# Low parts written over the raw weights, and rings of six raw and four high units, in a two-layer hybrid decoder

## The chip, the cores and the metric

The kernel runs on one core of one Trainium2 chip. A core has TensorE (PE in the profile; PEld is its loading of weights), VectorE (DVE), ScalarE (ACT), GpSimd (POOL), SyncE (SP, which here only starts transfers), 16 DMA engines, an on-chip memory for operands and eight banks for sums of products. The metric is the device time of one execution in microseconds (us), the median of three runs.

## The reference

Two decoder layers over 256 positions of width 2048, all float32:

```python
def reference(x, ...):
    for layer in range(2):
        xn = rms_norm(x, norm_mix[layer])
        if layer % 2 == 0:
            x = x + mixer_mlstm_ssd(xn, *mixer_params[layer])   # (xn @ w_in), mLSTM and SSD heads, then (mixed @ w_out)
        else:
            x = x + mixer_moba(xn, *mixer_params[layer])        # (xn @ w_qkv), attention, then (o @ w_o)
        x = x + swiglu(rms_norm(x, norm_ffn[layer]), *ffn_params[layer])
    return rms_norm(x, final_norm)

def swiglu(x, w_gate, w_up, w_down):
    return (jax.nn.silu(x @ w_gate) * (x @ w_up)) @ w_down
```

The weights are nearly all of the work: w_in is 2048 x 12336, w_out 4096 x 2048, w_qkv 2048 x 6144, w_o 2048 x 2048, and each layer has w_gate and w_up of 2048 x 5632 and w_down of 5632 x 2048.

## The kernel before

**Products.** TensorE multiplies in a rounded 32-bit form (fp32r). To keep float32 accuracy each operand is split into a high part (the rounded value) and a low part (the value less its high part), and a product is the sum of three: high by high, high by low, low by high (lines 479, 480 and 481 in `add`; 387 and 391 in `lin_w`; 417 to 419 in `lin_a`). One matmul is 128 x 128 by 128 x 512. Activations are split once and stay; weights are read once, in strips of 512 columns, and split as they come.

**What happens to a unit of weights.** In `block`, which does the gate z, w_out, the value columns of w_qkv, w_o and all of the two FFNs, a unit is four tiles of 128 x 512 (two row tiles of two strips, 8 KB a partition). `weights` (line 433) starts its two transfers of 512 KB on SyncE's queue into a `raw` buffer, ScalarE casts it to the high part `wh` (line 445) and VectorE subtracts that from `raw` into the low part `wl` (line 447), each in two pieces of 1024 columns. The letters of a plan say how each unit is multiplied. "P" is a plain unit: 24 matmuls. "S" is a unit of sums, seven products in place of eight: VectorE first makes four sums of the raw tiles (lines 454, 455, 457), which are a unit of their own in the raw ring; three of the raw tiles are split (one cast and one subtraction of 1536 columns), and all four sums (in two pieces of 1024 again); 21 matmuls follow. `chunks` (line 347) does the same for `lin_w` and `lin_a` in half units of 1024 columns.

**Rings.** From the stage z on the buffers are rings of three for each of `raw`, `wh` and `wl`, with one more raw buffer (`rawx`) for every fourth raw unit in the stages z, f and g (function `unit`, line 123). In the mixer the rings are four half units of raw and three each of `wh` and `wl`. A raw buffer is free for the next transfer once its cast and its subtractions are done; a `wh` or `wl` buffer once TensorE has read it.

**Order.** The kernel is written tile by tile, and the order on each engine is settled when it is built: an instruction goes where its dependencies and its priority put it (`tc.high_priority` moves casts, subtractions and evictions forward). Each engine then runs its list in order, and waits where an operand is not there.

**Stages.** m: the strips of w_in for the mLSTM and SSD heads, with the heads' own work between the strips. z: the gate columns of w_in, then w_out. f: FFN of layer 0. a: attention, w_qkv and w_o. g: FFN of layer 1. An FFN runs over its 11 strips of hidden columns in groups of 4, 4 and 3: `hidden` for each strip of the group (gate and up together), then `add_blocks` (line 918) for the group's part of w_down, twice 1024 output columns. The place where a group goes from its last hidden strip to w_down is called a seam here; there are six. At the end of a block's last unit of sums, lines 525 to 532 read the banks `acc_e` of the products into `pre`.

The lines that set the buffers before:

```python
MIXER = ({"raw": 4, "wh": 3, "wl": 3}, ...)
STAGING = tuple({tag: 1} for tag in "raw1 raw2 wh1 wh2 wl1 raw0 wh0 wl0 wl2".split())
...
    turn[kind] = turn.get(kind, -1) + 1
    return held_tile(f"{kind}{turn[kind] % 3}", shape, name, dt)
```

Of the kernel before, what the change touches and what calls it, by code (L numbers as in the profile page):

```python
# [43 lines left out]
STAGING = tuple({tag: 1} for tag in "raw1 raw2 wh1 wh2 wl1 raw0 wh0 wl0 wl2".split())  # L44
MIXER = ({"raw": 4, "wh": 3, "wl": 3}, {"cb": 1}, {"rows": 3}, {"hm": 2}, {"gap": 192}, {"ba": 4}, {"cols": 2}, {"wide": 2}, {"rb": 1})
JOIN = ({"rawx": 1}, {"gap": 256}, {"blk": 2})
FFN = ({"rawx": 1}, {"skh": 3}, {"blk": 4}, {"pre": 1})
ATTN = ({"blk": 4}, {"qk": 4}, {"v": 2}, {"rope": 1, "mask": 1}, {"rb": 1})
# [18 lines left out]
def hybrid_trunk(ctx: ExitStack, tc: tile.TileContext, a: dict, out: bass.AP):  # L67
# [8 lines left out]
    tmp = ctx.enter_context(tc.tile_pool(name="tmp", bufs=9))  # L76
    psm = ctx.enter_context(tc.tile_pool(name="psm", bufs=1, space=PSUM))
# [6 lines left out]
    staging = []  # L84

    def open_pool(name, pools):
        for i, tags in enumerate(pools):
            guard = tc.tile_pool(name=f"{name}{i}", bufs=1, reuse_waits="tile")
            pool = guard.__enter__()
            if "gap" in tags:  # L90
                pool.tile([P, tags["gap"] // 4], F32, name="gap")
            yield guard, pool, tags
# [6 lines left out]
    def open_stage(name, pools):  # L99
# [8 lines left out]
        stage["spare"] = any("rawx" in tags for tags in pools)  # L108

    def open_staging():  # L110

        close_stage()
        for guard, pool, tags in open_pool("st", STAGING):
            ctx.callback(guard.__exit__, None, None, None)
            staging.append((pool, tags))

    def held_tile(tag, shape, name, dt=F32):
        for pool, tags in stage["pools"] + staging:
# [4 lines left out]
    def unit(kind, shape, name, dt=F32):  # L123

        if not staging:
            return held_tile(kind, shape, name, dt)
        if kind == "raw" and stage["spare"]:
            turn["spare"] = turn.get("spare", -1) + 1
            if turn["spare"] % 4 == 3:
                return held_tile("rawx", shape, name, dt)  # L130
        turn[kind] = turn.get(kind, -1) + 1
        return held_tile(f"{kind}{turn[kind] % 3}", shape, name, dt)
# [214 lines left out]
    def chunks(w, col, nk, lead=None):  # L347

        n = 4 if staging else KC
        for k in range(0, nk, KC):  # L350
            if k % n == 0:
                raw = unit("raw", [P, n, STRIP], "raw")
                wh = unit("wh", [P, n, STRIP], "wh", F32R)
                wl = unit("wl", [P, n, STRIP], "wl", F32R)
# [888 lines left out]
```

## Time and profile before

| | |
|---|---|
| median of three runs | 2555.2 us (2554.48 to 2555.55) |
| span of the profiled execution | 2552.6 us |
| DMA packets | 507.49 MB, mean 199 GB/s |
| busy time of ScalarE | 1488.6 us (58%) |
| line 445, cast from raw, all shapes | 563 casts, 623.6 us |
| line 445, cast from sums | 250 casts, 256.9 us |
| line 447, low part from raw, all shapes | 563 subtractions, 740.5 us |
| line 447, low part from sums | 250 subtractions, 298.2 us |
| line 373, low part of half units | 223 subtractions, 269.6 us |
| lines 454, 455, 457, the sums of raw tiles | 125 of each; 152.1, 85.3 and 85.3 us |

The execution that was profiled has no time of its own beside its span; the 2.6 us between its span and the median of the runs are what lies around the span. A line of the profile names a group of instructions: source line, engine, operation, output and inputs, shape, count, busy time and mean duration in ns, and then the engine's idle time just before them with what ended it. Durations run from the start of an instruction to its last write, and two instructions on one engine overlap: what an instruction takes of its engine is the distance from its start to the next one's.

### The profile page before, as it was taken

How to read it: one execution, taken by the hardware profiler on the slowest of the kernel's cores; microseconds unless marked ns; L12 is line 12 of the kernel's file. 1: busy time of each engine (PE TensorE's matmuls, PEld its weight loads, DVE VectorE, ACT ScalarE, POOL GpSimd, SP SyncE). 2: the span in 40 equal slices, each digit the busy share in tenths (PEclk: the TensorE clock that was granted, in tenths of full speed). 3: DMA queues.
4: the chain of work that ended last, by engine and by line, in shares of the span. 5: the costliest groups of instructions: out<-in, count | busy, mean ns of one | idle time of the engine just before them, and what ended most of it. 6: DMA issues, size and time to landing. Idle time of an engine off the chain costs nothing.

```text
span 2552.6 us, 32527 instructions
## 1 busy us (share of the span) xinstructions
PE 2539.5 (99%) x12147; PEld 2122.4 (83%) x12147; DVE 2222.0 (87%) x2751; ACT 1488.6 (58%) x1960; POOL 55.7 (2%) x105
## 2 busy tenths in 40 slices
PE   9999999999999999999999999999999999999998
PEld 8888888888888888888888888888888888888887
DVE  5776778798989999999999987767999999999998
ACT  6455665566656655565555655666565545555555
POOL 1000010000000000000000000000000000000000
PEclk9999999999999999999999999999999999999999
DMA  8666576566565656565656557554556566665664
GB/s 291 176 208 185 164 230 185 167 205 214 181 214 177 221 188 218 203 223 174 230 191 222 195 173 231 165 165 147 195 181 219 191 213 207 211 201 198 223 205 165
DMA packets 257022, 507.49 MB, mean 199 GB/s; under 512 B 16104, under 2 KB 16256, under 8 KB 256352
## 3 DMA queue, kind: packets, MB, share of 16 engines
q1 hardware_dynamic: 249952, 483.20, 58.0%
q0 software_dynamic: 5616, 19.53, 2.2%
q10 hardware_dynamic: 1296, 2.69, 0.3%
q8 instruction: 95, 1.56, 0.2%
q14 instruction: 63, 0.52, 0.1%
HBM read 494.76 MB, written 2.14 MB: 195 GB/s over the span
## 4 chain that ended last, share of the span: by engine, by line
PE 95%; DVE 2%; issue 1%; ACT 1%; DMA 1%; SPq 0%; POOL 0%; POOLq 0%; ACTq 0%; DVEq 0%
PE acc_f L479 19%; PE acc_f L480 19%; PE acc_f L481 19%; PE acc_w L387 11%; PE acc_w L391 6%; PE acc_e L479 4%; PE acc_e L481 4%; PE acc_e L480 4%; PE acc_a L417 2%; PE acc_a L418 2%; PE acc_a L419 2%; PE p_tr L279 1%; PE p_y L891 1%; DVE wl L373 0%; PE p_num L768 0%
## 5 line engine op out<-in xcount | busy, mean ns | idle before, releaser
L445 ACT CAST wh<-raw 128x1024 fp32r<-128x1024 f32 (+1 forms) x563 | 623.6, 1147 | 384.0 <-PE acc_f L481 292.8
L447 DVE TENSOR_TENSOR wl<-raw,wh 128x1024 fp32r<-128x1024 f32 (+1 forms) x563 | 740.5, 1337 | 84.9 <-ACT wh L445 81.5
L479 PE MATMUL acc_f<-wh,x 128*128 128x512 f32 x1086 | 424.8, 391 | 0.5 <-DVE xres L928 0.5
L481 PE MATMUL acc_f<-wh,x 128*128 128x512 f32 x1086 | 422.9, 389 | 0.0
L480 PE MATMUL acc_f<-wl,x 128*128 128x512 f32 x1086 | 422.7, 389 | 0.0
L445 ACT CAST wh<-sums 128x1024 fp32r<-128x1024 f32 x250 | 256.9, 1052 | 282.5 <-PE acc_f L481 147.1
L373 DVE TENSOR_TENSOR wl<-raw,wh 128x1024 fp32r<-128x1024 f32 x223 | 269.6, 1222 | 128.9 <-ACT wh L372 125.2
L372 ACT CAST wh<-raw 128x1024 fp32r<-128x1024 f32 x223 | 230.6, 1048 | 183.7 <-PE acc_w L387 94.5
L447 DVE TENSOR_TENSOR wl<-sums,wh 128x1024 fp32r<-128x1024 f32 x250 | 298.2, 1218 | 10.6 <-ACT wh L445 9.8
L479 PEld LDWEIGHTS acc_f<-wh,x 128*128 128x128 f32 x1086 | 203.9, 188 | 43.9 <-DVE pre L1029 1.3
L481 PEld LDWEIGHTS acc_f<-wh,x 128*128 128x128 f32 x1086 | 203.9, 188 | 42.5
L480 PEld LDWEIGHTS acc_f<-wl,x 128*128 128x128 f32 x1086 | 203.9, 188 | 41.7
L387 PE MATMUL acc_w<-xa,wh 128*128 128x512 f32 x768 | 207.8, 398 | 1.2 <-DVE xa L222 1.1
L387 PEld LDWEIGHTS acc_w<-xa,wh 128*128 128x128 f32 x768 | 139.3, 189 | 27.4 <-ACT wh L365 1.4
L454 DVE TENSOR_TENSOR sums<-raw 128x1024 f32<-128x1024 f32 x125 | 152.1, 1217 | 8.4 <-DMA raw<-in_l_ffn_up 3.2
L387 PE MATMUL acc_w<-x,wh 128*128 128x512 f32 x512 | 139.2, 399 | 0.0
L391 PE MATMUL acc_w<-xa,wl 128*128 128x256 f32 x768 | 121.2, 283 | 0.0
L391 PEld LDWEIGHTS acc_w<-xa,wl 128*128 128x128 f32 x768 | 109.6, 190 | 6.5
L387 PEld LDWEIGHTS acc_w<-x,wh 128*128 128x128 f32 x512 | 92.5, 189 | 16.9
L479 PE MATMUL acc_e<-wh,skx 128*128 128x512 f32 x261 | 101.7, 391 | 0.0
L480 PE MATMUL acc_e<-wl,skx 128*128 128x512 f32 x261 | 101.6, 389 | 0.0
L481 PE MATMUL acc_e<-wh,skx 128*128 128x512 f32 x261 | 101.6, 389 | 0.0
(356 smaller groups left out, 4657.8 us busy)
## 6 DMA issues: line engine op xcount, KB each, us to landing
raw<-in_l_w_in SPq DMA_DIRECT2D x191, 512.0 KB, 3.7
raw<-in_l_ffn_gate SPq DMA_DIRECT2D x176, 512.0 KB, 4.0
raw<-in_l_ffn_up SPq DMA_DIRECT2D x176, 512.0 KB, 4.9
raw<-in_l_ffn_down SPq DMA_DIRECT2D x176, 512.0 KB, 5.0
raw<-in_l_w_qkv SPq DMA_DIRECT2D x96, 512.0 KB, 4.7
raw<-in_l_w_out SPq DMA_DIRECT2D x64, 512.0 KB, 5.0
raw<-in_l_w_o SPq DMA_DIRECT2D x32, 512.0 KB, 4.7
hr<-h POOLq DMA_DIRECT2D x32, 256.0 KB, 2.8
```

The costliest lines, as they stand in the source:

```text
L372: nc.scalar.copy(wh[:, ks, :], raw[:, ks, :])
L373: nc.vector.tensor_sub(wl[:, ks, :], raw[:, ks, :], wh[:, ks, :].bitcast(F32))
L387: return nc.tensor.matmul(banks[f], wh[:, kk, f * P:(f + 1) * P], kt.both(k0 + kk), start=k0 + kk == 0, stop=False, skip_group_check=True)
L391: nc.tensor.matmul(banks[f][:, :T], wl[:, kk, f * P:(f + 1) * P], kt.parts(k0 + kk)[0], start=False, stop=k0 + kk == nk - 1, skip_group_ch ...
L417: nc.tensor.matmul(banks[t], xh[:, ts], wh[:, kk, :], start=k0 + kk == 0, stop=False)
L418: nc.tensor.matmul(banks[t], xh[:, ts], wl[:, kk, :], start=False, stop=False)
L445: nc.scalar.copy(h[:, c, :], of[:, c, :])
L447: nc.vector.tensor_sub(l[:, c, :], of[:, c, :], h[:, c, :].bitcast(F32))
L454: nc.vector.tensor_sub(sums[:, 0:2, :], raw[:, 2:4, :], raw[:, 3:0:-2, :])
L479: nc.tensor.matmul(dst, ah, bh, start=start, stop=False)
L480: nc.tensor.matmul(dst, ah, bl, start=False, stop=False)
L481: nc.tensor.matmul(dst, al, bh, start=False, stop=stop)
```

## The change

There is one arena of 82,176 bytes a partition, and units lie at fixed places in it: the raw ring has six units, the `wh` ring four, and there is no `wl` ring. The low part is written over the raw weights, at the same addresses. A raw buffer is therefore held until TensorE has read the low part. One of the six raw units (`SPARE`) is in the ring in the stages z, f and g only; in stage a its place holds the first block of the attention's output, and attention keeps three `blk` buffers in place of four. In the mixer the same space is six half units of raw and four of `wh`; what the mixer keeps beside them (`cb`, `rows`, `hm`) has fixed places in the arena.

A plain unit's low part, and that of a unit of sums, is one subtraction of 2048 columns (line 462 now) in place of two of 1024; the casts stay in pieces of 1024. The three raw tiles of a unit of sums keep their one subtraction of 1536. The third instruction that makes sums (472 now, 457 before) stands before the first cast. Line numbers after the change are higher by 14 or 15 in what follows (479 to 481 are 494 to 496, 454 is 470, 1029 is 1043).

```diff
-STAGING = tuple({tag: 1} for tag in "raw1 raw2 wh1 wh2 wl1 raw0 wh0 wl0 wl2".split())
-MIXER = ({"raw": 4, "wh": 3, "wl": 3}, {"cb": 1}, {"rows": 3}, {"hm": 2}, {"gap": 192}, {"ba": 4}, {"cols": 2}, {"wide": 2}, {"rb": 1})
-JOIN = ({"rawx": 1}, {"gap": 256}, {"blk": 2})
-FFN = ({"rawx": 1}, {"skh": 3}, {"blk": 4}, {"pre": 1})
-ATTN = ({"blk": 4}, {"qk": 4}, {"v": 2}, {"rope": 1, "mask": 1}, {"rb": 1})
+ARENA, ARENA_END = 92672, 174848
+UNIT = 4 * STRIP * 4
+MIXER = ({"ba": 4}, {"cols": 2}, {"wide": 2}, {"rb": 1})
+JOIN = ({"blk": 2},)
+FFN = ({"skh": 3}, {"blk": 4}, {"pre": 1})
+ATTN = ({"blk": 3}, {"qk": 4}, {"v": 2}, {"rope": 1, "mask": 1}, {"rb": 1})
+CHUNKS = {"raw": range(6), "wh": range(6, 10)}
+UNITS = {"raw": (5, 7, 0, 1, 4, 9), "wh": (6, 2, 3, 8)}
+SPARE = 9
+PLACES = {"cb": (40960,), "rows": (47104, 53248, 59392), "hm": (65536, 73760)}
...
+    placed = {}
+    def place(name, offset, shape, dt=F32):
+        key = (name, offset, tuple(shape), dt)
+        if key not in placed:
+            placed[key] = nc.alloc_sbuf_tensor_at(f"{name}_at{offset}_{len(placed)}", list(shape), dt, offset=ARENA + offset).ap()
+        return placed[key]
...
-        stage["spare"] = any("rawx" in tags for tags in pools)
-    def open_staging():
-        close_stage()
-        for guard, pool, tags in open_pool("st", STAGING):
-            ctx.callback(guard.__exit__, None, None, None)
-            staging.append((pool, tags))
+        rings["small"] = name == "m"
+        rings["spare"] = name in ("z", "f", "g")
-        for pool, tags in stage["pools"] + staging:
+        if tag in PLACES:
+            turn[tag] = turn.get(tag, -1) + 1
+            return place(tag, PLACES[tag][turn[tag] % len(PLACES[tag])], shape, dt)
+        for pool, tags in stage["pools"]:
-    def unit(kind, shape, name, dt=F32):
-        if not staging:
-            return held_tile(kind, shape, name, dt)
-        if kind == "raw" and stage["spare"]:
-            turn["spare"] = turn.get("spare", -1) + 1
-            if turn["spare"] % 4 == 3:
-                return held_tile("rawx", shape, name, dt)
-        turn[kind] = turn.get(kind, -1) + 1
-        return held_tile(f"{kind}{turn[kind] % 3}", shape, name, dt)
+    rings = {"small": True, "spare": False}
+    for kind in CHUNKS:
+        rings[kind, True], rings[kind, False] = list(CHUNKS[kind]), list(UNITS[kind])
+    class Unit:
+        def __init__(self, kind):
+            ring = rings[kind, rings["small"]]
+            i = next(i for i in ring if rings["small"] or rings["spare"] or i != SPARE)
+            ring.remove(i)
+            ring.append(i)
+            self.kind, self.at = kind, i * (UNIT // 2 if rings["small"] else UNIT)
+        def part(self, cut, dt):
+            lo, hi = cut.start, cut.stop
+            return place(self.kind, self.at + lo * STRIP * 4, [P, hi - lo, STRIP], dt)
...
-        n = 4 if staging else KC
+        n = KC if rings["small"] else 4
-                raw = unit("raw", [P, n, STRIP], "raw")
-                wh = unit("wh", [P, n, STRIP], "wh", F32R)
-                wl = unit("wl", [P, n, STRIP], "wl", F32R)
+                raw_u, wh_u = Unit("raw"), Unit("wh")
+            raw, wl, wh = raw_u.part(ks, F32), raw_u.part(ks, F32R), wh_u.part(ks, F32R)
...
-                nc.sync.dma_start(raw[:, ks, :], rows)
+                nc.sync.dma_start(raw, rows)
-                    nc.scalar.copy(wh[:, ks, :], raw[:, ks, :])
-                    nc.vector.tensor_sub(wl[:, ks, :], raw[:, ks, :], wh[:, ks, :].bitcast(F32))
-            yield k, wh[:, ks, :], wl[:, ks, :]
+                    nc.scalar.copy(wh, raw)
+                    nc.vector.tensor_sub(wl, raw, wh.bitcast(F32))
+            yield k, wh, wl
...
     def weights(src, row, summed):
-        shape = [P, 4, STRIP]
-        raw = unit("raw", shape, "raw")
+        raw = Unit("raw")
+        pairs = slice(0, 2), slice(2, 4)
+        whole = raw.part(slice(0, 4), F32)
         for i, (w, col) in enumerate(src):
-            nc.sync.dma_start(raw[:, 2 * i:2 * i + 2, :],
+            nc.sync.dma_start(whole[:, pairs[i], :],
                               w[row:row + 2 * P, col:col + STRIP].rearrange("(a p) f -> p a f", p=P))
-        def parts(of, cuts):
-            h = unit("wh", shape, "wh", F32R)
-            l = unit("wl", shape, "wl", F32R)
-            for c in cuts:
-                nc.scalar.copy(h[:, c, :], of[:, c, :])
-            for c in cuts:
-                nc.vector.tensor_sub(l[:, c, :], of[:, c, :], h[:, c, :].bitcast(F32))
-            return h, l
+        def parts(of, n):
+            wh = Unit("wh")
+            x = of.part(slice(0, 4), F32)
+            h, l = wh.part(slice(0, n), F32R), of.part(slice(0, n), F32R)
+            for c in pairs if n == 4 else (slice(0, 3),):
+                nc.scalar.copy(h[:, c, :], x[:, c, :])
+            nc.vector.tensor_sub(l, x[:, :n, :], h.bitcast(F32))
+            return [(h[:, i, :], l[:, i, :]) for i in range(n)]
         with tc.high_priority(offset=800):
             if not summed:
-                return parts(raw, (slice(0, 2), slice(2, 4)))
-            sums = unit("raw", shape, "sums")
-            nc.vector.tensor_sub(sums[:, 0:2, :], raw[:, 2:4, :], raw[:, 3:0:-2, :])
-            nc.vector.tensor_sub(sums[:, 2, :], raw[:, 2, :], sums[:, 1, :])
-            first = parts(raw, (slice(0, 3),))
-            nc.vector.tensor_sub(sums[:, 3, :], raw[:, 0, :], sums[:, 2, :])
-            return first + parts(sums, (slice(0, 2), slice(2, 4)))
+                return parts(raw, 4)
+            sums = Unit("raw")
+            made = sums.part(slice(0, 4), F32)
+            nc.vector.tensor_sub(made[:, 0:2, :], whole[:, 2:4, :], whole[:, 3:0:-2, :])
+            nc.vector.tensor_sub(made[:, 2, :], whole[:, 2, :], made[:, 1, :])
+            nc.vector.tensor_sub(made[:, 3, :], whole[:, 0, :], made[:, 2, :])
+            return parts(raw, 3), parts(sums, 4)
     halved = slice(0, STRIP // 2), slice(STRIP // 2, STRIP)
...
-                wh, wl, sh, sl = weights(src, row + 2 * j * P, True)
+                own, made = weights(src, row + 2 * j * P, True)
-                b21, b11, b22 = [(wh[:, i, :], wl[:, i, :]) for i in range(3)]
-                t3, t1, t2_, t4 = [(sh[:, i, :], sl[:, i, :]) for i in range(4)]
+                b21, b11, b22 = [own[i] for i in range(3)]
+                t3, t1, t2_, t4 = [made[i] for i in range(4)]
...
-    oT = KT("o", KD)
+    oT = KT("o", KD, lambda shape, name, dt: place("o", SPARE * UNIT, shape, dt) if name == "o0" else blk(shape, name, dt))
```

VectorE in the sixth hidden strip of layer 0's FFN, where a unit of sums follows another unit; `ha` is the hidden activation, `sf` are sums of activations. Before:

```order
L454 TENSOR_TENSOR sums<-raw 128x1024
L220 TENSOR_TENSOR ha_9846<-xg,ha_9846 128x2x256
L455 TENSOR_TENSOR sums<-raw,sums 128x512
L309 TENSOR_TENSOR sf<-xg 128x128
L457 TENSOR_TENSOR sums<-raw,sums 128x512
L447 TENSOR_TENSOR wl<-raw,wh 128x1024 x2
L310 TENSOR_TENSOR sf<-xg 128x128
L311 TENSOR_TENSOR sf<-sf,xg 128x128
L1033 SCALAR_TENSOR_TENSOR h<-pre,r_6981,h 128x512
L447 TENSOR_TENSOR wl<-raw,wh 128x1536
L312 TENSOR_TENSOR sf<-xg,sf 128x128
L447 TENSOR_TENSOR wl<-sums,wh 128x1024 x2
```

The same place now, where each place of the arena has a name with a number of its own:

```order
L470 TENSOR_TENSOR raw_at_38_4532<-raw_at_34_4485 128x1024
L235 TENSOR_TENSOR ha_8743<-xg,ha_8743 128x2x256
L471 TENSOR_TENSOR raw_at_38_4532<-raw_at_34_4485,raw_at_38_4532 128x512
L324 TENSOR_TENSOR sf<-xg 128x128
L472 TENSOR_TENSOR raw_at_38_4532<-raw_at_34_4485,raw_at_38_4532 128x512
L325 TENSOR_TENSOR sf<-xg 128x128
L326 TENSOR_TENSOR sf<-sf,xg 128x128
L327 TENSOR_TENSOR sf<-xg,sf 128x128
L462 TENSOR_TENSOR raw_at_49_5194<-raw_at_34_4485,wh_at_40_4568 128x1536
L462 TENSOR_TENSOR raw_at_39_4535<-raw_at_38_4532,wh_at_42_4572 128x2048
```

The pair of 1024 columns that split the four sums has become one instruction of 2048, and the plain unit's pair that stood in the midst of the sums of activations stands ahead of this place now. Over the whole kernel 344 such pairs (219 plain units and 125 units of sums) became single instructions, and VectorE's list is shorter by these 344.

TensorE at the seam of the last group of layer 1's FFN, where the work goes from hidden strips (`skh` are the sums of their activations) to w_down's units (`hb82` is the last hidden activation). Before:

```order
L479 MATMUL acc_e_20585<-wh_20565,skh_20163 128x512
L480 MATMUL acc_e_20585<-wl_20566,skh_20163 128x512
L481 MATMUL acc_e_20585<-wh_20565,skh_20163 128x512
L479 MATMUL acc_e_20589<-wh_20565,skh_20163 128x512
L480 MATMUL acc_e_20589<-wl_20566,skh_20163 128x512
L481 MATMUL acc_e_20589<-wh_20565,skh_20163 128x512
...
L479 MATMUL acc_f_20513<-wh_20679,hb82_20544 128x512
L480 MATMUL acc_f_20513<-wl_20680,hb82_20544 128x512
```

The same seam now; `raw_at0_32` is the low part that lies over the raw weights of that place:

```order
L494 MATMUL acc_e_18304<-wh_at65536_42_4572,skh_17930 128x512
L495 MATMUL acc_e_18304<-raw_at8192_43_4637,skh_17930 128x512
L496 MATMUL acc_e_18304<-wh_at65536_42_4572,skh_17930 128x512
L494 MATMUL acc_e_18304<-wh_at24576_31_4434,skh_18187 128x512
L495 MATMUL acc_e_18304<-raw_at57344_29_4394,skh_18187 128x512
L496 MATMUL acc_e_18304<-wh_at24576_31_4434,skh_18187 128x512
L494 MATMUL acc_f_18235<-wh_at65536_42_4572,hb82_18266 128x512
L494 MATMUL acc_f_18248<-wh_at65536_42_4572,hb82_18266 128x512
L494 MATMUL acc_e_18505<-wh_at24576_40_4568,hb80_17913 128x512
L495 MATMUL acc_f_18235<-raw_at0_32_4435,hb82_18266 128x512
```

Now two units of sums are finished side by side, and the high unit at 65536 is read for the old unit in the third of these rows, cast anew, and its successor's low part is read six matmuls after that, in the last row.

VectorE and ScalarE at that seam, after the change, `pre` being the sums of products that are read out of the banks. ScalarE has:

```order
L540 COPY pre_18371<-acc_e_18292 128x512
L1179 DMA gf_18227<-in_final_norm 128x512 x2
L461 CAST wh_at65536_42_4572<-raw_at0_30_4431 128x1024 x2
L461 CAST wh_at24576_40_4568<-raw_at32768_34_4485 128x1536
L461 CAST wh_at16384_28_4393<-raw_at8192_33_4482 128x1024 x2
```

and VectorE has:

```order
L471 TENSOR_TENSOR raw_at40960_24_4346<-raw_at32768_34_4485,raw_at40960_24_4346 128x512
L472 TENSOR_TENSOR raw_at40960_24_4346<-raw_at32768_34_4485,raw_at40960_24_4346 128x512
L541 TENSOR_TENSOR pre_18372<-pre_18371,acc_e_18304 128x512
L462 TENSOR_TENSOR raw_at0_32_4435<-raw_at0_30_4431,wh_at65536_42_4572 128x2048
L542 TENSOR_TENSOR pre_18373<-pre_18372,acc_e_18296 128x512
```

So the subtraction that the tenth row of TensorE waits for comes after both casts and after L541, which reads the bank that TensorE fills until the sixth row.

More of the change, by code (lines that the diff above doesn't have):

```diff
@@ L76, in hybrid_trunk @@
     tmp = ctx.enter_context(tc.tile_pool(name="tmp", bufs=9))
+    arena = ctx.enter_context(tc.tile_pool(name="arena", bufs=1))
+    arena.tile([P, (ARENA_END - ARENA) // 4], F32, name="arena")
     psm = ctx.enter_context(tc.tile_pool(name="psm", bufs=1, space=PSUM))
@@ L83, in hybrid_trunk @@
     stage = {"guards": [], "pools": []}
-    staging = []
+    placed = {}
[4 more added lines that the diff above has]
+        return placed[key]
     def open_pool(name, pools):
@@ L89, in open_pool @@
             pool = guard.__enter__()
-            if "gap" in tags:
-                pool.tile([P, tags["gap"] // 4], F32, name="gap")
             yield guard, pool, tags
@@ L546, in block @@
                     for cut in halved if len(group) == lead == 2 and i == 3 else (slice(0, STRIP),):
-                        for jj, (wh, wl) in group:
+                        for jj, w in group:
                             for kk in range(2):
@@ L550, in block @@
                                 ts = slice(t * P, (t + 1) * P)
-                                add(F[i][:, cut], (xh[:, ts], xl[:, ts]), (wh[:, 2 * s + kk, cut], wl[:, 2 * s + kk, cut]),
+                                add(F[i][:, cut], (xh[:, ts], xl[:, ts]), tuple(part[:, cut] for part in w[2 * s + kk]),
                                     start=first and jj == group[0][0] and kk == 0,
@@ L969, in hybrid_trunk @@
         mixed.block(b)
-    open_staging()
     open_stage("z", JOIN)
```

## The prediction

> **What bounds the kernel now.** I read the page's busy times first, then the busy time of stretches, then the list of TensorE's waits, then single rows.
>
> ```profile
> span 2552.6 us, 32527 instructions
> PE 2539.5 (99%) x12147; PEld 2122.4 (83%) x12147; DVE 2222.0 (87%) x2751; ACT 1488.6 (58%) x1960; POOL 55.7 (2%) x105
> ```
>
> Two engines are candidates: TensorE at 99% and VectorE, which the change relieves, at 87%. The next view cuts the span into stretches; its columns are the stretch, its length, then the busy time (and instructions) of PE, PEld, DVE, ACT and POOL, the granted clock, the DMA share and GB/s.
>
> ```profile
> 0.00:64.00 64.00, 61.78 (x347) 54.24 (x348) 37.81 (x53) 39.86 (x67) 8.79 (x32) 1.00 0.85 291
> 768.00:1024.00 256.00, 256.00 (x1153) 210.91 (x1152) 243.06 (x268) 146.71 (x163) 3.99 (x7) 1.00 0.61 204
> 1024.00:1280.00 256.00, 256.00 (x1147) 211.06 (x1146) 240.87 (x248) 142.70 (x146) 3.22 (x6) 1.00 0.61 203
> 2500.00:2553.00 53.00, 43.53 (x203) 36.05 (x201) 46.25 (x62) 25.06 (x39) 1.12 (x2) 0.94 0.41 142
> ```
>
> In the FFN VectorE is busy 243.06 of 256 us, 95%, and TensorE all of them. In the first 64 us VectorE has 59%. So the question is whether TensorE is held back by VectorE in the FFN. Its busy share cannot say so, since matmuls overlap. Its pace can: here are four matmuls in the FFN (start, duration), and one piece of the chain that ended last, of eight matmuls, from the first 64 us.
>
> ```profile
> 899.62 0.39 PE L479 MATMUL acc_f<-wh,x 128*128 128x512 f32 x1
> 899.85 0.39 PE L480 MATMUL acc_f<-wl,x 128*128 128x512 f32 x1
> 900.07 0.39 PE L481 MATMUL acc_f<-wh,x 128*128 128x512 f32 x1
> 900.30 0.39 PE L479 MATMUL acc_f<-wh,x 128*128 128x512 f32 x1
> ...
> 59.87 1.84 PE acc_w L387 x8
> ```
>
> From 899.62 to 900.30 are three steps, 0.227 us each; 1.84 / 8 is 0.230. The pace is the same at 95% and at 59% of VectorE, so it is TensorE's own. What TensorE waited for, over all the span (total, times, longest):
>
> ```profile
> PE acc_w L387 <- DVE xa L222: 1.1, 1, 1.1
> PE p_idle L187 <- POOL alog L204: 1.0, 1, 1.0
> PE acc_f L479 <- DVE xres L928: 0.5, 1, 0.5
> PE acc_a L418 <- DVE wl L373: 0.5, 1, 0.5
> PE p_cols L705 <- ACT colsrc L692: 0.4, 1, 0.4
> ```
>
> That is 3.5 us in 2552.6, of which 0.5 us is for a low part. This is a kernel bound by TensorE nearly everywhere, and work taken from VectorE is worth only what it takes from those waits and from small delays that this list does not show.
>
> **The change part by part.** *The merged subtractions.* The order takes 344 instructions from VectorE. Their price comes from starts on VectorE:
>
> ```profile
> L447 DVE TENSOR_TENSOR wl<-raw,wh 128x1024 fp32r<-128x1024 f32 x438 | 522.7, 1219 | 83.2 <-ACT wh L445 80.1
> ...
> 1146.91 1.21 DVE L1029 TENSOR_TENSOR pre<-pre,acc_f 128x1024 f32<-128x1024 f32 x1
> 1148.05 0.68 DVE L457 TENSOR_TENSOR sums<-raw,sums 128x512 f32<-128x512 f32 x1
> 1148.65 0.68 DVE L220 TENSOR_TENSOR ha<-p_tr,ha 128x512 fp32r<-128x512 f32 x1
> ...
> 1155.86 2.35 DVE L447 TENSOR_TENSOR wl<-raw,wh 128x1024 fp32r<-128x1024 f32 x2
> 1158.13 0.28 DVE L310 TENSOR_TENSOR sf<-xg 128x128 f32<-128x128 f32 x1
> ...
> 1159.19 1.75 DVE L447 TENSOR_TENSOR wl<-raw,wh 128x1536 fp32r<-128x1536 f32 x1
> 1160.86 0.28 DVE L312 TENSOR_TENSOR sf<-xg,sf 128x128 f32<-128x128 f32 x1
> ```
>
> 512 columns take 0.60 us from start to start (1148.65 less 1148.05), a pair of 1024 takes 2.27 (1158.13 less 1155.86), 1536 take 1.67. The step per 512 is 0.535, so my estimate for 2048 is 2.20 us: a merge saves 0.07 us, 344 of them 24 us of VectorE. All of it lies beside TensorE's matmuls, so it is **0** in the sum. No row shows a subtraction written over one of its inputs, but an addition is: `pre<-pre,acc_f` of line 1029, at 1.14 us from start to start for 1024 columns, like half a pair of the subtraction (2.27 / 2). I take writing in place as free; it could not cost TensorE anything before it filled what VectorE has left.
>
> [...] The rows above have the next start 0.08 us before the listed end of the last one, so the trace gives 0.07.
>
> *The waits that may go.* With four high units and more raw ones, casts run further ahead. Now they wait for TensorE to release a high buffer:
>
> ```profile
> L445 ACT CAST wh<-raw 128x1024 fp32r<-128x1024 f32 (+1 forms) x563 | 623.6, 1147 | 384.0 <-PE acc_f L481 292.8
> raw<-in_l_ffn_down SPq DMA_DIRECT2D x176, 512.0 KB, 5.0
> ```
>
> In the order, the typical distance from the last matmul that read a high buffer to the first one that needs the next low part made from it grows from 21 to 24 matmuls (about 5 us) to 46 (10.4 us). Of the 3.5 us of waits the first two stand at the start, where the order hardly changes; I take half, **-1.8** (between -3.5 and 0).
>
> *The last seam.* At one place the distance shrinks: at the last seam of layer 1, to six matmuls, 6 x 0.227 = 1.36 us. The bank that L541 reads is finished three matmuls after the release (0.68 us, and 0.16 until the last write), L541 takes 0.60, and the subtraction of 2048 columns behind it takes 2.20 and 0.08 to its end: 3.7 us. The second of the two casts, 0.96 us, is done before that. TensorE stands still for 3.7 - 1.36 = **+2.4 us**. What the casts and line 541's forerunner (526) take:
>
> ```profile
> 1154.74 2.01 ACT L445 CAST wh<-raw 128x1024 fp32r<-128x1024 f32 x2 [3.44 <-PE acc_f L481]
> 1156.65 0.72 ACT L1032 ACTIVATE h<-pre,r 128x512 f32<-128x512 f32 x1
> ...
> 2502.13 0.69 DVE L526 TENSOR_TENSOR pre<-pre,acc_e 128x512 f32<-128x512 f32 x1
> 2502.73 1.22 DVE L447 TENSOR_TENSOR wl<-raw,wh 128x1024 fp32r<-128x1024 f32 x1
> ```
>
> Bounds: +0.5 if TensorE's part in line is later than I count, +3 if each hand-over costs 0.2 us more. This stall comes before the last w_down block, which runs dense to the end, so nothing takes it back.
>
> *The five other seams.* There the distance is 18 matmuls, 4.09 us. Two casts (1.91) and the subtraction (2.20) with its end and hand-overs take about 4.3, so **+0.2** each, +1.0. TensorE already loses time at such a place:
>
> ```profile
> 953.21 0.40 PE L480 MATMUL acc_f<-wl,ha 128*128 128x512 f32 x1
> ...
> 953.99 0.50 PE L479 MATMUL acc_e<-wh,skh 128*128 128x512 f32 x1
> 954.33 0.40 PE L480 MATMUL acc_e<-wl,skh 128*128 128x512 f32 x1
> ...
> 959.32 0.40 PE L479 MATMUL acc_f<-wh,ha 128*128 128x512 f32 x1
> ```
>
> From 953.21 to 959.32 are 25 matmuls, 6.11 us, against 25 x 0.227 = 5.68: 0.4 us lost, in pieces like the 0.34 from 953.99 to 954.33. Five seams lie between -2.0 (that loss goes) and +6 (one instruction of 1024 columns of VectorE stands ahead of each subtraction).
>
> *Transfers.* A raw buffer is now held until TensorE has read the low part. The shortest distance from that release to the need is 54 matmuls, 12.3 us, against a transfer of 5.0, two casts of 1.91 and a subtraction of 2.20 with hand-overs, 9.4 in all: **0**, with 2.9 us of cover; without it each such unit costs what it is late. The transfers themselves are as many and as large as before.
>
> *The tail.* TensorE's last matmuls do not move, and the additions and the norm behind them are untouched: **0**.
>
> **Sum**: -1.8 + 2.4 + 1.0 = +1.6 us, against the profiled execution's own 2552.6: a span of 2554.2, and with the 2.6 us around it (2555.2 less 2552.6) **2556.8**. The ends are -3.5 + 0.5 - 2.0 = -5.0 and +3 + 6 = +9, so 2550.2 to 2564.2. About 0.2% (5.1 us) is what a measurement of this kernel can tell from no change.
>
> **The rivals.** *VectorE is the real bound.* For it: 95% in the FFN, and TensorE's busy time is made of overlapping matmuls. Then the 24 us come back and the time is 2555.2 - 24 = 2531. Against it: the equal paces, and a list of waits with 0.5 us for low parts. [...]
>
> *The piece of 2048 comes too late at the seams (slower).* Before, TensorE could start on the first 1024 columns of a low part after 1.14 us; now it waits for all 2.20, and for what VectorE does ahead. With two of the three instructions that make sums ahead of it, 1.14 + 0.60 = 1.74 us, each of the five seams costs 1.9 in place of 0.2, 8.7 more: 2565.5. It decides where the subtraction starts more than 18 x 0.227 - 2.28 = 1.8 us after the release. For it: the order does put sums close by at seams. Against it: they need raw data that landed earlier and are mostly done by then.
>
> *Transfers late.* If a transfer takes 10 us in place of 5.0 where the cover is 2.9, a unit is 2.1 late; at one unit in each of the six groups +12.6, 2569. Against it: medians of 3.7 to 5.0, and a DMA share of 0.61.
>
> *The change does nothing of what it says.* The order shows the merged instructions and the longer distances, so what is left is that distances were never the limit: 2555.
>
> **Chances.** Forecast 0.70, VectorE as the bound 0.08, late pieces at the seams 0.15, late transfers 0.04, nothing 0.03. The forecast's own range, 2550 to 2564, holds 0.73 with the last; to leave out no more than 0.2 the range is drawn to 2567, which takes in the late pieces. Faster (below 2550.1): 0.08 and 0.02 of the forecast, 0.10. Slower (above 2560.3): 0.15, 0.04 and 0.02, 0.21. Same: 0.69.
>
> **What the changed profile would show.** VectorE's busy time near 2198 us with 344 fewer instructions; the subtraction of 2048 columns with a mean near 2.28 us; TensorE's pace in the FFN again 0.227 us; less idle time of casts behind TensorE; in the list of waits one for a low part of about 2.4 us, near 2500 us, and at most small ones at the other seams. If TensorE's pace becomes shorter than 0.227, I am wrong about the bound. If waits for low parts sum to more than 8 us, the seams are worse than I took them; if TensorE waits for a cast behind a transfer, the rings are too short.

## The result, and the profile after

The changed kernel takes 2574.3 us (2572.0 to 2575.1) against 2555.4 before on the same chip: a ratio of 1.0075, 95% interval 1.006 to 1.0089, **slower by 19 us**. The range was 2550 to 2567, so it does not hold the time. (One of the four executions of a control further down, that of five temporary buffers, took 13,967 us; its time is given as the median of the other three.) The page after has, for the span and the busy times:

```profile
span 2573.2 us, 33020 instructions
PE 2544.8 (99%) x12147; PEld 2124.7 (83%) x12147; DVE 2210.4 (86%) x2407; ACT 1495.2 (58%) x1960; POOL 60.0 (2%) x105
```

and, among the groups with shapes kept apart, the merged low part (line 462):

```profile
L462 DVE TENSOR_TENSOR raw_at<-raw_at,wh_at 128x2048 fp32r<-128x2048 f32 x344 | 781.4, 2286 | 85.4 <-ACT wh_at L461 82.9
```

The 344 merged subtractions are there and last 2.286 us. TensorE's share still reads 99%: a busy time made of matmuls that last 0.39 us and start 0.227 us apart, as in the rows below, hides short stops. Its pace has not moved: from the first to the last of these are three steps, 0.68 us, 0.227 each.

```profile
1511.18 0.39 PE L494 MATMUL acc_f<-wh_at,x 128*128 128x512 f32 x1
...
1511.86 0.39 PE L494 MATMUL acc_f<-wh_at,x 128*128 128x512 f32 x1
```

So the time went into stops. The list of TensorE's waits (total, times, longest) is 3.5 us before; its largest rows now are:

```profile
PE acc_e L494 <- DVE hb L235: 3.9, 2, 3.2
PE acc_w L401 <- DVE qT L439: 2.8, 1, 2.8
PE acc_f L494 <- DVE xres L943: 2.2, 1, 2.2
PE p_tr L292 <- issue: 1.9, 4, 0.9
PE acc_f L494 <- DVE pre L1043: 1.6, 2, 1.4
PE acc_f L495 <- DVE raw_at L462: 1.6, 2, 1.0
PE p_rb L357 <- DVE dg L356: 1.5, 1, 1.5
```

Only the row of line 462 is a low part. Five others are **hand-offs**, work of VectorE that TensorE needs before it can go on: the split of a turned hidden activation (235), the read-out of query, residual or `pre` banks (439, 943, 1043), a scaling for the row norm (356). The row with "issue" names nobody; each of its four stops ends 0.1 us after a read-out of `acc_e` banks (544), so it is of the same kind. Where in the span the loss arises shows when the start of the k-th matmul of one trace is set against that of the other (both have 12147):

```text
matmul      250   3500   3750   7250   9250   9750  11750  12000  12147
before     47.1  680.9  735.8 1513.6 1898.0 2009.4 2457.6 2512.4 2543.2
after      51.6  684.2  741.6 1522.9 1908.0 2022.0 2469.7 2533.1 2563.8
behind     +4.5   +3.3   +5.8   +9.3  +10.1  +12.6  +12.1  +20.8  +20.5
```

Two places make 13 of the 20.5 us: 4.5 in the first 50 us, and 8.7 at the last seam. Small ones at 685, 860 to 1010, 1514 and 1942 to 1980 us make the rest in this trace.

**The first place.** VectorE of the changed kernel, and the ScalarE cast that the second low part (387) waits for (in square brackets the idle time before an instruction, and what ended it):

```profile
30.34 1.22 DVE L387 TENSOR_TENSOR raw_at<-raw_at,wh_at 128x1024 fp32r<-128x1024 f32 x1 [1.57 <-ACT wh_at L386]
31.49 0.42 DVE L439 TENSOR_TENSOR qT<-acc_w,qT 128x256 f32<-128x256 f32 x1
33.12 1.23 DVE L387 TENSOR_TENSOR raw_at<-raw_at,wh_at 128x1024 fp32r<-128x1024 f32 x1 [1.22 <-ACT wh_at L386]
34.27 0.74 DVE L439 TENSOR_TENSOR qT<-acc_w,qT 128x256 f32<-128x256 f32 x2
...
32.04 1.04 ACT L386 CAST wh_at<-raw_at 128x1024 fp32r<-128x1024 f32 x1 [1.47 <-DMA raw_at<-in_l_w_in]
```

TensorE needs the banks that the second `qT` row empties. That row (34.27) stands behind a low part, which waits for a cast, which waits for a transfer. No matmul is late for its own weights here, and still TensorE stands:

```profile
31.68 0.40 PE L401 MATMUL acc_w<-xa,wh_at 128*128 128x512 f32 x1
34.83 1.55 PE L401 MATMUL acc_w<-xa,wh_at 128*128 128x512 f32 x4 [2.75 <-DVE qT L439]
```

From 31.68 to 34.83 us it starts nothing, 2.9 us more than a step; then it runs at a lower clock, as windows over it show (columns as in the prediction; after POOL's comes the granted clock):

```profile
32.00:35.00 3.00, 0.25 (x2) 0.20 (x2) 1.88 (x3) 1.59 (x3) 0.00 (x0) 1.00 0.31 121
35.00:38.00 3.00, 3.00 (x11) 2.53 (x11) 0.90 (x3) 1.42 (x2) 0.00 (x0) 0.57 0.00 0
```

**The last seam.** Here the chain that ended last (start, duration, what) runs through a transfer, which is the piece to see:

```profile
2507.19 7.23 DMA raw_at<-in_l_ffn_down
...
2514.54 1.23 DVE raw_at L470
2515.76 0.61 DVE hb L235
...
2516.51 0.47 PE acc_e L494
2516.98 0.38 PE acc_e L495
2517.36 0.43 PE acc_e L496
...
2519.17 0.09 DVE pre L541
...
2519.78 2.29 DVE raw_at L462
...
2522.11 0.50 PE acc_f L495
```

The split of the last hidden activation (235) could not run before 2515.7, because the sums of raw weights (470) stand ahead of it on VectorE and wait for their transfer until 2514.4. TensorE waited 3.22 us, then ran at 0.43 us a matmul; from 2519.17 on follows the stall that the prediction had priced.

### The profile page after: what moved, and what is told of

It reads as the page before. It is cut to its first block, busy times and chain, and to the rows that moved or that the text cites. A ratio compares the mean times of both kernels' runs of the same rounds, so it can differ in the third digit from the quotient of the medians.

```text
span 2573.2 us, 33020 instructions
## 1 busy us (share of the span) xinstructions
PE 2544.8 (99%) x12147; PEld 2124.7 (83%) x12147; DVE 2210.4 (86%) x2407; ACT 1495.2 (58%) x1960; POOL 60.0 (2%) x105
## 4 chain that ended last, share of the span: by engine, by line
PE 93%; DMA 3%; DVE 2%; issue 1%; ACT 1%; SPq 0%; POOLq 0%; POOL 0%; DVEq 0%; ACTq 0%
PE acc_f L494 18%; PE acc_f L495 18%; PE acc_f L496 18%; PE acc_w L401 11%; PE acc_w L405 6%; PE acc_e L494 4%; PE acc_e L495 4%; PE acc_e L496 4%; PE acc_a L431 2%; PE acc_a L433 2%; PE acc_a L432 2%; PE p_tr L294 1%; PE p_y L906 1%; DMA raw_at<-in_l_ffn_down 1%; DMA raw_at<-in_l_w_qkv 1%
## 5 line engine op out<-in xcount | busy, mean ns | idle before, releaser
L461 ACT CAST wh_at<-raw_at 128x1024 fp32r<-128x1024 f32 (+1 forms) x813 | 887.5, 1118 | 679.0 <-PE acc_f L496 412.3
L462 DVE TENSOR_TENSOR raw_at<-raw_at,wh_at 128x2048 fp32r<-128x2048 f32 (+1 forms) x469 | 996.3, 2145 | 96.6 <-ACT wh_at L461 88.5
L494 PE MATMUL acc_f<-wh_at,x 128*128 128x512 f32 x1086 | 424.5, 391 | 1.7 <-DVE pre L1043 1.6
L496 PE MATMUL acc_f<-wh_at,x 128*128 128x512 f32 x1086 | 422.8, 389 | 0.0
L495 PE MATMUL acc_f<-raw_at,x 128*128 128x512 f32 x1086 | 422.7, 389 | 0.0
L387 DVE TENSOR_TENSOR raw_at<-raw_at,wh_at 128x1024 fp32r<-128x1024 f32 x223 | 272.1, 1223 | 144.1 <-ACT wh_at L386 142.2
L386 ACT CAST wh_at<-raw_at 128x1024 fp32r<-128x1024 f32 x223 | 233.4, 1049 | 192.1 <-PE acc_w L401 120.8
L494 PEld LDWEIGHTS acc_f<-wh_at,x 128*128 128x128 f32 x1086 | 203.9, 188 | 44.7 <-DVE pre L1043 2.5
L496 PEld LDWEIGHTS acc_f<-wh_at,x 128*128 128x128 f32 x1086 | 203.9, 188 | 42.5
L495 PEld LDWEIGHTS acc_f<-raw_at,x 128*128 128x128 f32 x1086 | 203.9, 188 | 41.7
L401 PE MATMUL acc_w<-xa,wh_at 128*128 128x512 f32 x768 | 209.2, 399 | 3.4 <-DVE qT L439 2.8
L494 PE MATMUL acc_e<-wh_at,skx 128*128 128x512 f32 x261 | 101.7, 390 | 0.1
L496 PE MATMUL acc_e<-wh_at,skx 128*128 128x512 f32 x261 | 101.6, 389 | 0.0
```

The costliest lines, as they stand in the source:

```text
L386: nc.scalar.copy(wh, raw)
L387: nc.vector.tensor_sub(wl, raw, wh.bitcast(F32))
L401: return nc.tensor.matmul(banks[f], wh[:, kk, f * P:(f + 1) * P], kt.both(k0 + kk), start=k0 + kk == 0, stop=False, skip_group_check=True)
L461: nc.scalar.copy(h[:, c, :], x[:, c, :])
L462: nc.vector.tensor_sub(l, x[:, :n, :], h.bitcast(F32))
L494: nc.tensor.matmul(dst, ah, bh, start=start, stop=False)
```

## The experiments

All ratios are to the kernel before on the same chip. "Casts on transfers" is the sum of ScalarE's waits in which a cast waits for a raw transfer: 24 us before, 125 in the changed kernel (the expectations say 20 and 110 or 113, from the larger rows alone). Three theories were set against each other first: late transfers, behind which casts, sums and read-outs queue (A); the long piece, which blocks VectorE (B); another order of the same work, by chance (C).

**Pairs again, rings as changed.**

```diff
-            nc.vector.tensor_sub(l, x[:, :n, :], h.bitcast(F32))
+            for c in pairs if n == 4 else (slice(0, 3),):
+                nc.vector.tensor_sub(l[:, c, :], x[:, c, :], h[:, c, :].bitcast(F32))
```

> The changed kernel with its rings, but each low part of 2048 columns again made by two subtractions of 1024. Theory A (raw buffers are held until TensorE has read the low part, so transfers start late and in bursts, and casts, sums and evictions queue behind them): the time stays near the changed kernel's 2574, 2568 to 2580, and ScalarE's casts still wait for transfers for about 110 us in all, against about 20 before. Theory B (the 2.2 us pieces block VectorE): it returns to 2555 to 2562. Theory C (only another order of the same work, by chance): it may land anywhere from 2555 to 2580, and not with the number of late transfers.

Measured: 2572.1, ratio 1.0071 (1.0054 to 1.0088), where the changed kernel has 1.0075. VectorE is busy 2237.5 us in place of 2210.4, so the merge does take 27 us off VectorE, and the time does not answer. The loss is not the merge's in these rings; B falls for the changed kernel. Casts wait for transfers 111 us here, as A said.

**The merge alone, in the rings of before.**

```diff
-            for c in cuts:
-                nc.vector.tensor_sub(l[:, c, :], of[:, c, :], h[:, c, :].bitcast(F32))
+            c = slice(cuts[0].start, cuts[-1].stop)
+            nc.vector.tensor_sub(l[:, c, :], of[:, c, :], h[:, c, :].bitcast(F32))
```

> The kernel before with its rings of three, but with one subtraction of 2048 columns for a plain unit and a unit of sums. Theory A: within 5 us of before, 2551 to 2560, casts wait for transfers for about 20 us as before. Theory B: 2563 or more, with TensorE waiting for evictions that stand behind a subtraction. Theory C: anywhere.

Measured: 2582.0, ratio 1.0113 (1.0098 to 1.0128), 28.6 us slower, though casts wait for transfers only 12 us. A's number is wrong and B's holds here, but by another wait than B named: TensorE waits for the weights themselves, not for evictions.

```profile
PE acc_f L480 <- DVE wl L447: 5.9, 7, 2.1
PE acc_e L479 <- ACT wh L445: 5.3, 15, 1.3
PE acc_e L480 <- DVE wl L447: 4.3, 6, 1.3
```

With three high units, a unit's casts start when TensorE releases one, about 21 matmuls (4.8 us) before the low part is needed; two casts (1.91 together) and a piece of 2.20 leave 0.7 us for everything else, where a first piece of 1.14 left 1.8. So the long piece needs the fourth high unit, which the next run supports.

**Seven raw and three high units; five raw and four high units.**

```diff
-UNITS = {"raw": (5, 7, 0, 1, 4, 9), "wh": (6, 2, 3, 8)}
+UNITS = {"raw": (5, 7, 0, 1, 4, 9, 8), "wh": (6, 2, 3)}
...
+UNITS = {"raw": (5, 7, 0, 1, 9), "wh": (6, 2, 3, 8)}
```

> The changed kernel with seven raw units and three high units in place of six and four. Theory A: raw buffers come free for the next transfer earlier against the need, so the casts wait less for transfers (below 80 us) and the time falls, to 2556 to 2570. Theory B: unchanged, 2570 to 2578. Theory C: anywhere, without a bond to the transfers.

> The changed kernel with five raw units instead of six (four high units as in it; one unit of the arena stays empty). Theory A: transfers later still, casts wait for them for more than 150 us, and the time rises above 2585. Theory B: unchanged, 2570 to 2578. Theory C: anywhere, without a bond to the transfers.

Measured: 2600.1, ratio 1.0183 (1.0168 to 1.0198), and 2590.8, ratio 1.0144 (1.0129 to 1.0159). Casts wait for transfers 23 us with seven raw units and 437 us with five, against 125 with six: the size of the raw ring sets how late transfers are, as A said. With five units the time rose as A said too (above 2585), but with seven it should have fallen and rose further. With seven, TensorE waits for low parts again, as the merge did with three high units:

```profile
PE acc_f L495 <- DVE raw_at L462: 11.4, 17, 1.3
```

With five it waits for read-outs:

```profile
PE acc_f L494 <- DVE xres L943: 7.3, 9, 1.3
PE acc_f L494 <- DVE pre L1043: 6.3, 9, 1.1
```

The seven also cost a high unit, so two things changed at once; a next pair of runs parted them.

**Seven raw and four high units, and their control.** The place comes from the temporary buffers.

```diff
-    tmp = ctx.enter_context(tc.tile_pool(name="tmp", bufs=9))
+    tmp = ctx.enter_context(tc.tile_pool(name="tmp", bufs=5))
...
-UNITS = {"raw": (5, 7, 0, 1, 4, 9), "wh": (6, 2, 3, 8)}
+UNITS = {"raw": (5, 7, 0, 1, 4, 9, 10), "wh": (6, 2, 3, 8)}
```

> The changed kernel with seven raw units and four high units; the place comes from five temporary buffers in place of nine. If raw buffers that are held until TensorE has read the low part are what makes the casts late: casts wait for transfers below 60 us (against about 113), and the time falls by the part of the loss that comes from them, to 2556 to 2568, less what five temporary buffers cost (the next kernel). If the loss is only order: no bond between the two, 2568 to 2580.

> The changed kernel with five temporary buffers in place of nine and 8 KB left empty: what the place for the seventh raw unit costs by itself. 2574 to 2582.

Measured: 2607.6, ratio 1.0211 (1.0196 to 1.0226), and for the control 2570.9, ratio 1.0069 (1.0052 to 1.0086): the place for the seventh unit costs nothing. Casts wait for transfers only 46 us, as A said, but the kernel is some 36 us *slower* than the control, which neither side of the expectation had. More raw units let VectorE prepare weights earlier, and the order of the build puts that work ahead of the read-outs. VectorE at one end of a hidden strip:

```profile
859.35 2.28 DVE L462 TENSOR_TENSOR raw_at<-raw_at,wh_at 128x2048 fp32r<-128x2048 f32 x1
861.55 0.68 DVE L542 TENSOR_TENSOR pre<-pre,acc_e 128x512 f32<-128x512 f32 x1
862.15 1.22 DVE L470 TENSOR_TENSOR raw_at<-raw_at 128x1024 f32<-128x1024 f32 x1
863.29 1.22 DVE L544 TENSOR_TENSOR pre<-pre,acc_e 128x1024 f32<-128x1024 f32 x1
864.42 2.28 DVE L462 TENSOR_TENSOR raw_at<-raw_at,wh_at 128x2048 fp32r<-128x2048 f32 x1
866.62 2.35 DVE L1043 TENSOR_TENSOR pre<-pre,acc_f 128x1024 f32<-128x1024 f32 x2
```

Nothing here waits for a transfer: weight work of the next units (462, 470, 462) is simply ahead, and TensorE waits for line 1043, which reads the `acc_f` banks:

```profile
867.89 0.50 PE L494 MATMUL acc_f<-wh_at,x 128*128 128x512 f32 x1 [1.96 <-DVE pre L1043]
```

In its list of waits that row stands with 10.4 us, six times; a row of 8.0 us that names nobody (`p_tr`, four stops) ends each time 0.1 us after a read-out of line 544. The granted clock is at half for eight stretches of 3.4 us, against two in the control; at 1.7 us each (half of 3.4, an estimate) the six more are some 10 of the 36 us. The last section comes back to them. This fells A as the one cause: late transfers are one thing that can hold VectorE's list ahead of a hand-off, and early weights are another. What counts is what stands ahead of the hand-off. The next experiments moved hand-offs alone.

**The mixer's rings as before.**

```diff
-CHUNKS = {"raw": range(6), "wh": range(6, 10)}
+CHUNKS = {"raw": range(4), "wh": range(4, 7), "wl": range(7, 10)}
...
-            raw, wl, wh = raw_u.part(ks, F32), raw_u.part(ks, F32R), wh_u.part(ks, F32R)
+            raw, wl, wh = raw_u.part(ks, F32), wl_u.part(ks, F32R), wh_u.part(ks, F32R)
```

> The changed kernel, but in the mixer the half units have the rings of before (four raw, three high, three low of their own at fixed places); nothing else differs. In the changed kernel TensorE stands still at 31.7 us for 2.9 us behind a query eviction that follows a low part on VectorE, and runs at a lower clock for the next 3 us: 4.5 us in all up to 50 us. If the mixer's rings set that order and that wait: 2567 to 2572, with the first 50 us as before, and the rest as in the changed kernel. If it was chance or lay in other loads: 2572 to 2577.

Measured: 2570.1, ratio 1.0064 (1.0049 to 1.0079), against 1.0075: 3 us less, with intervals that overlap. The trace is plainer: at the 250th matmul this kernel is 0.3 us behind before, in place of 4.5 (in the profiled execution its last seam costs 11.2 us in place of 8.7). The first place is the mixer's rings: with those of before, VectorE has three `qT` read-outs ahead of the low part that stands at 33.12 us in the changed kernel, which has one there. The second is at 29.50 us in place of 34.27:

```profile
28.64 0.42 DVE L440 TENSOR_TENSOR qT<-acc_w,qT 128x256 f32<-128x256 f32 x1
29.50 0.42 DVE L440 TENSOR_TENSOR qT<-acc_w,qT 128x256 f32<-128x256 f32 x1 [0.44 <-ACT qT L439]
31.43 1.22 DVE L388 TENSOR_TENSOR wl_at<-raw_at,wh_at 128x1024 fp32r<-128x1024 f32 x1 [1.50 <-ACT wh_at L387]
```

This trace shows one thing more. From 592 us on, TensorE, VectorE and ScalarE run the same instructions in the same order as in the changed kernel, and yet this trace loses 3.0 us between matmuls 3500 and 9750, where that of the changed kernel loses 9.3. So, but for the one at 685 us, which both have, the small stops between the two places come and go under the same order, and these traces cannot put a single one of them down to the change. The last seam stays in these traces: 8.7 us in the changed kernel, 9.1 with pairs, 8.5 in the control with five temporary buffers, 11.2 here.

**Splits of hidden activations first.**

```diff
-        with tc.high_priority(offset=1200 if kt.name in ("x1", "x2", "x3") else 0):
+        with tc.high_priority(offset=1200 if kt.name[0] in "xh" else 0):
```

> The changed kernel, but the splits of the turned hidden activations have priority 1200 in place of 0, so that on VectorE they stand ahead of sums that wait for a transfer. At the last seam of layer 1 both splits now stand ahead of the sums (L470) of the next unit. If hand-offs behind waiting sums cost the most there (3.6 and 1.0 us of stillness and some 1.8 us of lower clock): 6 us less there, 2564 to 2571 in all. If late transfers alone set the time there, whatever the order: 2571 to 2577.

Measured: 2560.2, ratio 1.0021 (1.0012 to 1.0031), 0.0054 or 14 us less, more than expected. Casts wait for transfers 123 us, as in the changed kernel: the transfers are as late, and it no longer matters. At the last seam VectorE runs both splits ahead of the sums:

```profile
2497.22 1.28 DVE L235 TENSOR_TENSOR hb<-p_tr,hb 128x512 fp32r<-128x512 f32 x2
...
2511.07 1.22 DVE L470 TENSOR_TENSOR raw_at<-raw_at 128x1024 f32<-128x1024 f32 x1
```

and TensorE has no stop there; from the first to the last of these are 93 steps of 0.227 us:

```profile
2498.79 0.39 PE L494 MATMUL acc_e<-wh_at,skh 128*128 128x512 f32 x1
...
2519.90 0.39 PE L496 MATMUL acc_f<-wh_at,hb 128*128 128x512 f32 x1
```

Between matmuls 11750 and 12000 it loses 0.1 us to before, in place of 8.7. The edit also changes TensorE's order at the seam (the work on the last activation comes sooner), so the 2.4 us that the prediction had there go with it. In the traces the rest is some 5 us between matmuls 3500 and 9750. Much of it is in the stops that come and go, so it is not shown to be the priority's. Between the kernel just above and that just below, which differ by the priority alone, the traces differ by 10.7 us, and the last seam makes 11.1.

**Both edits.** The priority line and the mixer's rings together; nothing else.

> The changed kernel with the mixer's rings of before and the splits of hidden activations at priority 1200: the two edits that took 4.2 and 14.1 us each by itself. If the loss sits in single places where a hand-off stands behind other work on VectorE, the two add up: 2574.3 - 4.2 - 14.1 = 2556, 2553 to 2559. If it is one common cause that either of them relieves, the sum fails: 2560 or more.

Measured: 2556.2, ratio 1.0011 (1.0002 to 1.0019), as the sum says. Of the 0.0075 that the change lost, 0.0064, some 16 of 19 us, go with two edits that touch neither the merge nor the rings from stage z on. Of the three theories that leaves the order, but not by chance: what counts is which hand-off stands behind what.

**All turned activations and the row norm's scaling first.** On top of both edits:

```diff
-        with tc.high_priority(offset=1200 if kt.name[0] in "xh" else 0):
+        with tc.high_priority(offset=1200):
...
-            nc.vector.tensor_scalar(dg, ident, r[:, t:t + 1], None, op0=OP.mult)
+            with tc.high_priority(offset=1200):
+                nc.vector.tensor_scalar(dg, ident, r[:, t:t + 1], None, op0=OP.mult)
```

> As the one before, with the splits of all turned activations (the gated output's too) and the row norm's scaling at priority 1200. The places at 685 and 1512 us, of 1.6 and 0.8 us, should go: 2551 to 2557, below before (2553.8) or level with it. If priorities only shift the waits elsewhere: 2556 or more.

Measured: 2555.7, ratio 1.0006 (0.9997 to 1.0015): level with before, not below it. Of the stop at 685 us 0.5 us is left; that at 1512 us was gone already with both edits.

**Both edits, with pairs again.** The diff of the first experiment on top of both edits.

> The kernel of both edits with each 2048-column low part made in two subtractions of 1024 again: what the merge is worth in the new rings when the worst hand-offs are out of the way. If VectorE's 24 us are off the path and a piece of 2.2 us costs nothing with four high units: within 3 us of the kernel of both edits. If the long piece still delays evictions: 3 to 8 us faster than it.

Measured: 2560.2, ratio 1.0023 (1.0014 to 1.0033): 4.0 us slower than with the merge (their intervals just overlap), outside either expectation. So the merge is worth a little in these rings, or the order that comes with it is; one pair of kernels cannot tell.

**The priority alone, on the kernel before.** The same line of `transpose_split` in the kernel before.

> The kernel before with the splits of hidden activations at priority 1200 and nothing else. Its last seam has no such wait, so within 4 us of before: 2550 to 2558. If the priority by itself is worth the 14 us that it took from the changed kernel: 2540 to 2545.

Measured: 2557.2, ratio 1.0015 (1.0006 to 1.0024). The priority is no gain by itself; it takes away a wait that before does not have.

## Why the prediction was wrong

**The bound** was right. TensorE's pace stayed 0.227 us while VectorE lost 344 instructions, and 27 us more on VectorE (pairs against merge) left the ratio at 1.0071 against 1.0075.

**The merged subtractions** were right in their price: 2.286 us against an estimate of 2.28 to the end, and 27 us of VectorE against 24, at no cost in place. VectorE's busy time is 2210.4 us all the same, not 2198: with pairs the new rings have 2237.5 where before had 2222.0.

**The last seam** was right as far as it went. The row of 2518.86 us (two matmuls) is followed by stops of 0.71 us for a cast and 0.99 us for the low part:

```profile
2518.86 1.05 PE L494 MATMUL acc_f<-wh_at,hb 128*128 128x512 f32 x2
2520.63 0.50 PE L494 MATMUL acc_e<-wh_at,hb 128*128 128x512 f32 x1 [0.71 <-ACT wh_at L461]
2522.11 0.50 PE L495 MATMUL acc_f<-raw_at,hb 128*128 128x512 f32 x1 [0.99 <-DVE raw_at L462]
```

From 2518.86 to 2522.11 are three steps, 3.25 us; less 3 x 0.227 that is 2.6, where +2.4 was predicted, by the chain that was named (L541, then the piece of 2.2 us). That the two are so close is partly luck: TensorE ran at half clock just before (0.43 us a matmul in place of 0.227), which delayed L541's bank, and the stop for a cast was not in the sum.

**The step that failed** is "Transfers: 0, with 2.9 us of cover". It compared a transfer, two casts and a subtraction with the time until TensorE needs *that low part*. That cover held: the row for low parts (462) is 1.6 us in all. What it left out is who else stands behind an instruction that waits for the transfer. At the last seam, VectorE's list has the sums of a raw unit (470) between the two splits of the last activation (235), and the transfer took 7.2 us in place of 5.0. Two rows of VectorE's order further up than those that were shown would have shown that place. The same was left out at the start, where a low part of the mixer's half units stands ahead of a `qT` read-out; the prediction took the order there as hardly changed. The rival of late pieces had sums standing in front, and set them aside: they were said to need raw data that landed earlier. At the last seam their data landed at 2514.4 us, after TensorE had stopped. In the rival of late transfers (0.04) the wait was put in the low part too, so its 2569 came nearest of the cases without their mechanism being the true one.

**The waits that may go** (-1.8) hardly did: of the two rows at the start, 2.1 us of the 3.5, 1.7 us are still in the list after, and new waits came beside them.

**What lies around the span** was taken as 2.6 us, from a span and a median of different executions. For one and the same execution after the change it is 1.8 (2575.0 less 2573.2), so that term was 0.8 too large.

**The five other seams** (+1.0) are too small to be read apart from their surroundings; the largest stop found at one of them is 0.75 us (at 967.6 us), the others are below 0.3, against 0.2 each in the sum.

**The rival of late pieces at seams** (0.15) had a true mechanism in the wrong kernel: it is what the merge costs with three high units, 28.6 us, and with the fourth unit pairs and merge are level (1.0071 and 1.0075).

Open: what makes the small stops between the two places come and go, what the last 0.0011 is made of, and whether the 4.0 us between merge and pairs with both edits are the merge's or its order's.

## What to carry to other kernels

On an engine that runs its list in order, as VectorE did in these traces, a deeper ring is not only cover: it lets preparation be placed ahead of hand-offs, and each such place then waits as long as the preparation's own input is late (TensorE stood 3.22 us at the last seam), or as long as the preparation itself runs (1.96 us for line 1043 with seven raw and four high units). Go through the list of each engine for read-outs and splits that TensorE waits for, and ask of what stands ahead of them, not only of the operand that was moved, what it waits for and how long it runs. Give such hand-offs a higher priority than preparation when a ring is deepened. In the kernel before, the same priority gained nothing, and here it only took the loss back: TensorE's own pace of 0.227 us was the bound, and no run with the deeper rings is faster than before.

## What the hardware showed that was not expected

A stop of TensorE can cost more than its length. After the stops of 2.75 us at 31.7 and 3.22 us at 2512.9 (as the waits list them) the granted clock was 0.57 in the three us from 35 on, and 0.65 here:

```profile
2516.00:2519.00 3.00, 2.49 (x7) 1.99 (x8) 1.66 (x3) 1.04 (x1) 0.00 (x0) 0.65 0.07 13
```

A matmul then takes 0.43 us in place of 0.227. After the first stop 16 matmuls, eight of 512 columns and eight of 256, lie between 34.83 and this row:

```profile
39.25 1.08 PE L401 MATMUL acc_w<-xa,wh_at 128*128 128x512 f32 x4
```

That is 4.42 us. In the chain of before, eight of 512 take 1.84 us (the prediction's row) and eight of 256 columns take 0.95:

```profile
61.71 0.95 PE acc_w L391 x8
```

So 4.42 - 2.79 = 1.6 us came on top of the 2.9.

The length of a stop alone does not decide this. In the kernel with seven raw and four high units, a stop of 1.66 us is followed by half clock (the first two rows, from 945 us) and a stop of 2.68 us is not (the last two, from 34 us):

```profile
945.03:948.44 3.41, 1.75 (x13) 1.35 (x12) 3.41 (x5) 0.92 (x2) 0.00 (x0) 1.00 0.01 4
948.44:951.86 3.42, 3.42 (x9) 2.67 (x8) 3.42 (x3) 1.82 (x4) 0.00 (x0) 0.50 0.00 0
...
33.74:37.15 3.41, 2.01 (x11) 1.77 (x12) 2.01 (x4) 1.34 (x3) 0.00 (x0) 1.00 0.01 5
37.15:40.56 3.41, 3.41 (x22) 3.03 (x21) 2.45 (x2) 1.39 (x3) 0.00 (x0) 1.00 0.68 169
```

The windows are 3.41 us long because the clock of these traces changes on such a grid: in the changed kernel it goes to half at 35.42 and 2516.91 us, which is 727 times 3.413 us apart, and each time back 3.41 us later. With each of the fourteen traces cut along its own grid, leaving out the ends, all 17 windows in which TensorE's matmuls leave 1.8 us or more idle are followed by a window at half clock, and none at full clock with 1.62 us or less is; of the seven in between (1.66 to 1.76) three are. So beside its length it counts where a stop lies on the grid: the stop of 2.68 us falls into two windows, with 1.4 us of idle time in the second.
